# Moving one-operand work of an RWKV-7 / GLA encoder's recurrences from VectorE to ScalarE

## The chip, the cores and the metric

The kernel runs on one core of one Trainium2 chip. The metric is the device time of one execution in microseconds (us). TensorE (PE, with its weight loads PEld) multiplies, VectorE (DVE), ScalarE (ACT) and GpSimd (POOL) do elementwise work, and SyncE (SP) issues the transfers (DMA). Each engine takes its instructions in the order in which its list has them.

## The reference

One encoder layer is applied to two sequences, of 512 and 256 tokens, with 1024 channels in fp32. The mixer is the part that matters here: half of its channels go through an RWKV-7 recurrence (8 heads of 64, in both directions), half through gated linear attention (GLA, 4 heads, in both directions). A memory attention and a feed-forward layer follow.

```python
def rwkv7_scan(r, w, k, v, kk, a):               # per head, state S of 64 x 64
    def step(S, inp):
        r_t, w_t, k_t, v_t, kk_t, a_t = inp
        sa = jnp.einsum('bhij,bhj->bhi', S, -kk_t)
        S = (S * w_t[:, :, None, :] + sa[..., None] * (kk_t * a_t)[:, :, None, :]
             + v_t[..., None] * k_t[:, :, None, :])
        return S, jnp.einsum('bhij,bhj->bhi', S, r_t)
...
    kk = hd(k * p['k_k'])                        # scaled keys, then normalised per head
    kk = kk * lax.rsqrt(jnp.sum(kk * kk, axis=-1, keepdims=True) + 1e-12)
...
    a = jax.nn.sigmoid(a0 + ad @ a2)
    kd = hd(k * (1.0 + (a - 1.0) * k_a))         # decayed key, per direction
...
def encoder_trunk(x, mem, params):
        x = x + rms_norm(hybrid_mixer(rms_norm(x, p['g_mix_pre']), p), p['g_mix_post'])
        m = rms_norm(mem, p['g_mem'])
        x = x + rms_norm(cross_attention(rms_norm(x, p['g_x_pre']), m, p), p['g_x_post'])
        h = rms_norm(x, p['g_ffn_pre'])
        x = x + rms_norm(jnp.square(jax.nn.relu(h @ p['w_ff1'])) @ p['w_ff2'], p['g_ffn_post'])
```

## The kernel before

The 768 tokens stand side by side in tiles of 128 channels. A product in fp32 is made of three passes: each operand is split into a high part (ACT, L149) and a rest (DVE, L150), and `mm3` (L249) sums three products. A dense block is 128 columns of a weight: four transfers `wraw`, four splits `whi` and `wlo`, then 24 matmuls of 512 columns and 24 of 256, and an evacuation by ACT (L482 for GLA, L322 with two DVE passes L324 and L327 for the RWKV inputs). The tiles of the splits hold one block, so a block's splits follow the matmuls of the block before.

The recurrence is cut into chunks of 64 tokens and worked on by pairs of heads p = 0 to 3:

- `begin(p)`: `prep` makes the scaled and normalised key `kk` (L704, L705, head sums, L706 to L708). For each direction d `decays` makes the cumulated decays (L649 or L651 by a scan, L653, L655) and the decayed key (L659, L661, L662); `bk_of`, `ar_of` and `lower` make the chunk matrices (`low`, evacuated by L695) and send them through HBM.
- `invert(p)`: `inverses` loads 48 + 48 lower triangles of 32x32 (`sn`, `sx`), turns the second half end to end (L746), does 31 column steps on DVE (a product L752 and a sum L754 each), and stores the results: direct, transposed (L756, L760) and turned (L758).
- `joined(p)`: `join` loads these blocks (`tt`, `tdz`) and makes the 64x64 inverses by two products on PE (L796 with its copy L800, L808 with its copy L811).
- `stage(q)`: `step` runs the recurrence itself over chunks (L1046 to L1077), with `products` ahead of it.

Beside it run the four GLA heads (`gla_head(h)`, L848 to L947: decays, score products L872 `gs`, turn L885, states L900 and the DVE chain L911, outputs L923 and L925, store to `mixd`), the dense blocks and, after 1296 of their matmuls, the blocks of the memory (`memory_block`). `tokens_first` turns a 128-channel tile to tokens first, by PE, and copies the result to SBUF (L472).

The order is set by the framework: it gives every instruction a priority by its place in the program, raised in `tc.high_priority(offset=...)`, simulates all engines with a cost model, and writes down each engine's list in the order in which the simulation ran it. So an instruction that changes its engine can move others on all engines. Each list is then fixed, and a waiting instruction holds up what stands behind it. All transfers are issued by SP, from one list.

Of the kernel before, what the change touches and what calls it, by code (L numbers as in the profile page):

```python
# [10 lines left out]
AF = mybir.ActivationFunctionType  # L11
ALU = mybir.AluOpType
# [20 lines left out]
def kernel(ctx: ExitStack, tc: tile.TileContext, I, y_prompt, y_sample):  # L33
    nc = tc.nc
    act = nc.scalar
    dve = nc.vector
# [262 lines left out]
    ka1 = cp.tile([P, 4], F32, name="ka1")  # L299
# [15 lines left out]
    def cvc(name, i=0):  # L315
        return cv[:, col[name] + i:col[name] + i + 1]
# [73 lines left out]
    for v in ("w0_f", "w0_b", "a0_f", "a0_b", "k_k", "k_a", "lnx_w", "lnx_b"):  # L390
# [11 lines left out]
                      op0=ALU.mult, op1=ALU.add)  # L402
# [61 lines left out]
    def tokens_first(ot):  # L464

        vt = gd2("gd")
        for c, n in SEQS:
            pt = psd("gvt")
            for j in range(0, n, P):
                pe.transpose(out=pt[:, j:j + P], in_=ot[:, c + j:c + j + P], identity=ident)  # L470
            with tc.high_priority():
                dve.tensor_copy(out=vt[:, c:c + n], in_=pt[:, 0:n])  # L472
        return vt.rearrange("p (j e) -> p j e", e=P)

    def gla_dense(g, i):
# [12 lines left out]
    if True:  # L488
# [72 lines left out]
        with tc.high_priority(offset=3000):  # L561
            for p in range(4):
                cs = slice(p * P, (p + 1) * P)
                for kind in (0, 2):
                    ots = [lp.tile([P, T], F32, tag="lo", bufs=6, name="lo_t") for _ in range(2)]
                    wt, xt = (w2s, xw) if kind < 2 else (a2s, xa)
                    for c0, n in SEQS:
# [3 lines left out]
                        for d in range(2):  # L571
                            sigm = act.activation(out=ots[d][:, c0:c0 + n], in_=pts[d][:, 0:n], func=AF.Sigmoid,
                                                  bias=cvc(("w0_f", "w0_b", "a0_f", "a0_b")[kind + d], p))
# [4 lines left out]
                for c0, n in SEQS:  # L578
                    pt, pz = psy("lops"), psy("gzps")
# [16 lines left out]
        for i in range(4):  # L596
# [3 lines left out]
            for k0 in range(0, KD, 4):  # L600
                pt = psm("ptr")
# [23 lines left out]
    sn, sq, sx = snf[0:112], sqf[0:112], sxf[0:112]  # L625
# [16 lines left out]
    def decays(st, d):  # L642

        p = st["p"]
        wa = pt_("wa")
        dma(wa, lora[p, d])
        cum = pt_("wb")
        if d == 0:
            dve.tensor_tensor_scan(out=cum, data0=scan_mask, data1=wa, initial=0.0, op0=ALU.mult, op1=ALU.add)  # L649
        else:  # L650
            dve.tensor_tensor_scan(out=cum[:, ::-1], data0=scan_mask, data1=wa[:, ::-1], initial=0.0,  # L651
                                   op0=ALU.mult, op1=ALU.add)
        act.activation(out=px_at, in_=v3(cum), func=AF.Exp, scale=-E_HALF)  # L653
        pinv = pt_("wa")
        act.activation(out=pinv, in_=cum, func=AF.Exp, scale=E_HALF)  # L655
        wc = pt_("wc")
        dma(wc, lora[p, 2 + d])
        nka = pt_("wb")
        dve.scalar_tensor_tensor(out=nka, in0=wc, scalar=-1.0, in1=st["kk"], op0=ALU.mult, op1=ALU.mult)  # L659
        kd = st["kds"] if d == 0 else wc  # L660
        dve.tensor_scalar(out=wc, in0=wc, scalar1=cvc("k_a", p), scalar2=ka1[:, p:p + 1], op0=ALU.mult, op1=ALU.add)  # L661
        dve.tensor_tensor(out=kd, in0=wc, in1=st["k"], op=ALU.mult)  # L662
        return pinv, nka, kd

# [35 lines left out]
    def prep(st):  # L700

        p = st["p"]
        kk, wa = pt_("kk", 2), pt_("wa")
        act.activation(out=wa, in_=st["k"], func=AF.Square, scale=cvc("k_k", p))  # L704
        dve.tensor_scalar(out=kk, in0=st["k"], scalar1=cvc("k_k", p), scalar2=None, op0=ALU.mult)  # L705
        head_sums(wa, lambda c0, n, pt: act.activation(out=wa[:, c0:c0 + n], in_=pt[:, 0:n], func=AF.Ln, bias=eps_kk))  # L706
        act.activation(out=wa, in_=wa, func=AF.Exp, scale=-0.5)
        dve.tensor_tensor(out=kk, in0=kk, in1=wa, op=ALU.mult)  # L708
        st["kk"] = kk
        st["r"] = pt_("r")  # L710
        dma(st["r"], rkvd[p, 1])
        st["kds"] = pt_("kds")
        st["lts"] = []

        pcs = st["pcs"] = mp.tile([P, 6, 4], F32, tag="pcs", bufs=4, name="pcs")
        for d in range(2):
            pinv, nka, kd = decays(st, d)
            b_ = bk_of(pinv, nka, kd)
            to_places(bkd[p], b_, d)
            a_ = ar_of(st, d)  # L720
            to_places(ard[p], a_, d)
            lower(st, d, b_, a_)
            if d == 1:
                dve.tensor_tensor(out=st["kds"], in0=st["kds"], in1=kd, op=ALU.add)
            last = px[:, :, 1 if d else 64].rearrange("p (q c) -> p q c", c=2)
            for c, n in ((0, 6),) if d == 0 else ((0, 4), (4, 2)):
                o = pcs[:, c:c + n, 2 * d:2 * d + 2]
                pool.tensor_scalar(out=o[:, ::-1] if d else o, in0=last[:, c:c + n], scalar1=1.0, scalar2=None, op0=ALU.mult)
# [10 lines left out]
    def inverses(st):  # L739


        flat = fl
        ld, qd, td = (x[st["p"]] for x in (lds, qds, tds))
        dma(sn[0:48], ld[0].rearrange("s b c t -> (b c) s t"))
        dma(sx[64:112], ld[1].rearrange("s b c t -> (b c) s t"))
        dve.tensor_copy(out=flat(sn[64:112]), in_=flat(sx[64:112])[:, ::-1])  # L746
        dve.memset(sq, 0.0)
        dve.memset(flat(sq)[:, 0:1024:33], 1.0)
        for j in range(31):
            nr, ni = j + 1, 31 - j  # L750
            tm = stmp[:, 0:nr * ni].rearrange("p (a b) -> p a b", a=nr)
            dve.tensor_tensor(out=tm, in0=sq[:, 0:nr, j:j + 1].broadcast_to([112, nr, ni]),  # L752
                              in1=sn[:, j:j + 1, j + 1:32].broadcast_to([112, nr, ni]), op=ALU.mult)
            dve.tensor_tensor(out=sq[:, 0:nr, j + 1:32], in0=sq[:, 0:nr, j + 1:32], in1=tm, op=ALU.add)  # L754
        dma(qd[0].rearrange("s b c t -> (b c) s t"), sq[0:48])
        dve.tensor_copy(out=sn[0:48], in_=sq[0:48].rearrange("p a b -> p b a"))  # L756
        dma(td[0].rearrange("s b c t -> (b c) s t"), sn[0:48])
        dve.tensor_copy(out=flat(sx[64:112]), in_=flat(sq[64:112])[:, ::-1])  # L758
        dma(qd[1].rearrange("s b c t -> (b c) s t"), sx[64:112])
        dve.tensor_copy(out=sn[64:112], in_=sq[64:112, ::-1, ::-1].rearrange("p a b -> p b a"))  # L760
        dma(td[1].rearrange("s b c t -> (b c) s t"), sn[64:112])
    def begin(p, k_=None):
        if k_ is None:
# [16 lines left out]
    def join(st):  # L780
        qd, td = qds[st["p"]], tds[st["p"]]
        tt, lts = tts, st["lts"]
# [7 lines left out]
        for d in range(2):  # L790
            o0, o1 = 32 * d, 32 - 32 * d
# [10 lines left out]
        for d in range(2):  # L802
            o0, o1 = 32 * d, 32 - 32 * d
            pn = psn("merge2")[:, 0:NCH * 32].rearrange("p (c x) -> p c x", x=32)
            for c in range(NCH):
                for h in (0, 64):
                    ks_ = slice(h + o1, h + o1 + 32)
                    pe.matmul(out=pn[h + o0:h + o0 + 32, c, :], lhsT=fts[d][ks_, c, :], rhs=tt[d][ks_, c, o1:o1 + 32],  # L808
                              start=True, stop=True)
            for h in (0, 64):  # L810
                dve.tensor_copy(out=tt[d][h + o0:h + o0 + 32, :, o1:o1 + 32], in_=pn[h + o0:h + o0 + 32])  # L811
            to_places(ttd[st["p"]], tt[d], d)

    def blocks(bs):
# [518 lines left out]
    with tc.tile_pool(name="ao", bufs=1, reuse_waits="tile") as ao:  # L1333
# [18 lines left out]
        for h in range(4):  # L1352
# [16 lines left out]
            for s_, (c0, n) in enumerate(SEQS):  # L1369
# [19 lines left out]
                for m in range(2):  # L1389
                    pt = psm("xt")  # L1390
# [95 lines left out]
    with tc.tile_pool(name="f1", bufs=1, reuse_waits="tile") as f1, tc.tile_pool(name="fw", bufs=1, reuse_waits="tile") as fw:  # L1486
# [98 lines left out]
        h = {"11": blk[0][0], "21": blk[1][0], "22": blk[1][1], "t1": blk[0][1]}  # L1585
# [185 lines left out]
```

## Time and profile before

| | us |
|---|---|
| median of 3 runs | 1554.85 |
| lowest and highest of the runs | 1549.77 and 1558.52 |
| the profiled execution, its own time | 1548.75 |
| span of the profile, first to last instruction | 1546.6 |
| busy PE, weight load, DVE, ACT, POOL | 1408.3, 1183.6, 1076.7, 706.0, 220.9 |
| mean granted TensorE clock | 0.930 of full speed |

The times in the profile count from the span's start. "Busy" counts an engine's instructions and not its waits; a row's "idle before" names what ended a wait. The first preparation starts at some 118 us, the fourth inversion ends at some 650 us, and the mixer's output product starts at some 787 us.

### The profile page before, as it was taken

Reading aid. Unit: us, or ns where it says so; the run is one execution under the profiler, and the core shown is the slowest. Engines: PE = TensorE matmul, PEld = TensorE weight load, DVE = VectorE, ACT = ScalarE, POOL = GpSimd, SP = SyncE. Lnnn points to the kernel's source line nnn. Section 1 sums busy time; section 2 is a strip of 40 time slices with the busy share of each in tenths; the row PEclk is TensorE's granted clock in tenths of the full one; section 3 lists DMA queues with packets and bytes.
Section 4 is the critical chain, followed back from the end, with each engine's and each line's share of the span. In section 5 each row is a group of like instructions: output and inputs, shape, how many; then the busy total and the mean of one; then the engine's idle time right before and its main releaser. Section 6 shows DMA issues by size and latency. Waiting matters only on the chain.

```text
span 1546.6 us, 27578 instructions
## 1 busy us (share of the span) xinstructions
PE 1408.3 (91%) x10238; PEld 1183.6 (77%) x10238; DVE 1076.7 (70%) x1913; ACT 706.0 (46%) x1477; POOL 220.9 (14%) x304
## 2 busy tenths in 40 slices
PE   7998899897799987999699999978999999999996
PEld 6886778775676766777478887868999998787785
DVE  5555896698567994866665554279766667788886
ACT  5664345443423442344353454345554555454342
POOL 5301000000000000003211233320000002132132
PEclk9999899987779996799799999988999999999998
DMA  6687666584468667464452332244554547555334
GB/s 165 177 314 210 171 197 156 167 228 102 128 187 232 180 184 168 106 166 144 128 179 98 107 100 79 82 154 155 196 170 153 181 157 291 155 175 172 120 103 136
DMA packets 279562, 250.30 MB, mean 162 GB/s; under 512 B 89264, under 2 KB 227059, under 8 KB 279428
## 3 DMA queue, kind: packets, MB, share of 16 engines
q1 hardware_dynamic: 279428, 248.54, 53.8%
q8 instruction: 81, 1.33, 0.4%
q14 instruction: 53, 0.43, 0.1%
HBM read 164.11 MB, written 82.58 MB: 160 GB/s over the span
## 4 chain that ended last, share of the span: by engine, by line
PE 59%; DVE 13%; DMA 11%; issue 8%; SPq 3%; ACT 3%; POOL 2%; DVEq 0%; ACTq 0%; POOLq 0%
PE pd L249 19%; PE fx L1548 7%; PE gx L1548 6%; PE fz L1548 5%; PE gz L1548 5%; SPq L41 3%; PE po L249 3%; DMA wraw<-in_w_in_dram 1%; DVE ws L1488 1%; PE hsum L639 1%; DVE wl L1539 1%; DMA raw<-in_w_out_dram 1%; PE xo L249 1%; POOL rs L1264 1%; PE bktp L1028 1%
## 5 line engine op out<-in xcount | busy, mean ns | idle before, releaser
L249 PE MATMUL pd<-hT_hi,whi 128*128 128x256 f32 (+1 forms) x512 | 183.5, 358 | 9.1 <-DVE gd L327 4.1
L249 PE MATMUL pd<-hT_lo,whi 128*128 128x256 f32 (+1 forms) x512 | 180.2, 352 | 0.3 <-DVE hT_lo L208 0.3
L249 PE MATMUL pd<-hT_hi,wlo 128*128 128x256 f32 (+1 forms) x512 | 178.5, 350 | 0.0
L149 ACT ACTIVATE whi<-wraw 128x256 fp32r<-128x256 f32 x192 | 77.5, 415 | 97.2 <-PE pd L249 59.4
L249 PEld LDWEIGHTS pd<-hT_hi,whi 128*128 128x128 f32 x512 | 100.9, 197 | 24.0 <-DVE gd L327 4.0
L150 DVE TENSOR_TENSOR wlo<-wraw,whi 128x256 fp32r<-128x256 f32 x192 | 80.2, 437 | 48.2 <-ACT whi L149 46.6
L249 PEld LDWEIGHTS pd<-hT_lo,whi 128*128 128x128 f32 x512 | 101.0, 197 | 13.1 <-DVE hT_lo L208 0.5
L249 PEld LDWEIGHTS pd<-hT_hi,wlo 128*128 128x128 f32 x512 | 100.2, 196 | 13.2 <-issue 0.5
L150 DVE TENSOR_TENSOR ul<-ur,uh 128x768 fp32r<-128x768 f32 x56 | 75.3, 1351 | 30.2 <-ACT uh L149 17.7
L149 ACT ACTIVATE uh<-ur 128x768 fp32r<-128x768 f32 x56 | 47.2, 845 | 106.6 <-PE gz L1548 51.8
L1538 ACT ACTIVATE wh<-w 128x1024 fp32r<-128x1024 f32 x64 | 67.1, 1053 | 36.7 <-PE fz L1548 24.2
L1539 DVE TENSOR_TENSOR wl<-w,wh 128x1024 fp32r<-128x1024 f32 x56 | 68.2, 1217 | 15.3 <-ACT wh L1538 14.7
L1548 PE MATMUL gx<-wh,uh 128*128 128x512 f32 x192 | 74.9, 397 | 4.2 <-DVE acc L1741 4.2
L1548 PE MATMUL gx<-wl,uh 128*128 128x512 f32 x192 | 75.9, 395 | 0.0
L1548 PE MATMUL gx<-wh,ul 128*128 128x512 f32 x192 | 75.4, 395 | 0.0
L1539 POOL TENSOR_TENSOR wl<-w,wh 128x1024 fp32r<-128x1024 f32 x8 | 20.9, 2610 | 329.3 <-ACT wh L1538 329.3
L1548 PE MATMUL fz<-hh,wh 128*128 128x384 f32 x192 | 66.1, 344 | 1.7 <-ACT wh L1538 1.7
L1548 PE MATMUL fz<-hl,wh 128*128 128x384 f32 x192 | 65.9, 343 | 0.0
L1548 PE MATMUL fz<-hh,wl 128*128 128x384 f32 x192 | 65.2, 344 | 0.6 <-DVE wl L1539 0.6
L1538 ACT ACTIVATE wh<-ws 128x1024 fp32r<-128x1024 f32 x48 | 50.5, 1052 | 27.2 <-PE fx L1548 22.5
L1548 PE MATMUL gz<-wl,uh 128*128 128x512 f32 x144 | 56.9, 395 | 0.0
L249 PE MATMUL pd<-mem_hi,wlo 128*128 128x512 f32 x128 | 56.0, 439 | 0.9 <-DVE wlo L150 0.9
(537 smaller groups left out, 3980.4 us busy)
## 6 DMA issues: line engine op xcount, KB each, us to landing
w<-in_w_ff_dram SPq DMA_DIRECT2D x64, 512.0 KB
ur<-ud SPq DMA_DIRECT2D x56, 384.0 KB
wraw<-in_w_in_dram SPq DMA_DIRECT2D x108, 128.0 KB
ud<-u SPq DMA_DIRECT2D x32, 384.0 KB
ud<-us SPq DMA_DIRECT2D x24, 384.0 KB
wraw<-in_wkv_x_dram SPq DMA_DIRECT2D x64, 128.0 KB
lora<-lo_t SPq DMA_DIRECT2D x20, 384.0 KB
bkg<-bkd SPq DMA_DIRECT2D x24, 256.0 KB
```

Source lines behind the costliest of these rows:

```text
L41: return nc.sync.dma_start(out=out, in_=in_)
L149: act.activation(out=hi, in_=src, func=AF.Copy)
L150: (lo_eng or pool).tensor_tensor(out=lo, in0=src, in1=hi, op=ALU.subtract)
L249: pe.matmul(out=out, lhsT=a, rhs=b, start=(i == 0), stop=(i == n - 1))
L639: pe.matmul(out=pt[:, 0:n], lhsT=ones_bd, rhs=src[:, c0:c0 + n], start=True, stop=True)
L1028: pe.transpose(out=pt[:, u, :], in_=fl(b_[HS[h], u]), identity=ident[HS[h], HS[h]])
L1264: pool.tensor_tensor(out=rs, in0=ms, in1=neg_half, op=ALU.pow)
L1488: dve.tensor_tensor(out=out, in0=a, in1=b, op=ALU.subtract)
L1538: act.activation(out=hi, in_=t[name], func=AF.Copy)
L1539: lo_eng.tensor_tensor(out=lo, in0=t[name], in1=hi, op=ALU.subtract)
L1548: pe.matmul(out=out, lhsT=a, rhs=b, start=first and i == 0, stop=last and i == n - 1, skip_group_check=True)
```

## The change

Eight lines of five functions are written for ACT instead of DVE. Seven copies, of which four read or write turned or transposed, are ACT's Copy; the scaled key is Copy with a column as scale; the decayed key's factor is Identity with a column as scale and one as bias. Shapes, tiles, transfers and results are the same; no table is loaded more often.

```diff
 tokens_first:
-                dve.tensor_copy(out=vt[:, c:c + n], in_=pt[:, 0:n])
+                act.activation(out=vt[:, c:c + n], in_=pt[:, 0:n], func=AF.Copy)
 decays:
-        dve.tensor_scalar(out=wc, in0=wc, scalar1=cvc("k_a", p), scalar2=ka1[:, p:p + 1], op0=ALU.mult, op1=ALU.add)
+        act.activation(out=wc, in_=wc, func=AF.Identity, scale=cvc("k_a", p), bias=ka1[:, p:p + 1])
 prep:
-        dve.tensor_scalar(out=kk, in0=st["k"], scalar1=cvc("k_k", p), scalar2=None, op0=ALU.mult)
+        act.activation(out=kk, in_=st["k"], func=AF.Copy, scale=cvc("k_k", p))
 inverses:
-        dve.tensor_copy(out=flat(sn[64:112]), in_=flat(sx[64:112])[:, ::-1])
+        act.activation(out=flat(sn[64:112]), in_=flat(sx[64:112])[:, ::-1], func=AF.Copy)
...
-        dve.tensor_copy(out=sn[0:48], in_=sq[0:48].rearrange("p a b -> p b a"))
+        act.activation(out=sn[0:48], in_=sq[0:48].rearrange("p a b -> p b a"), func=AF.Copy)
...
-        dve.tensor_copy(out=flat(sx[64:112]), in_=flat(sq[64:112])[:, ::-1])
+        act.activation(out=flat(sx[64:112]), in_=flat(sq[64:112])[:, ::-1], func=AF.Copy)
...
-        dve.tensor_copy(out=sn[64:112], in_=sq[64:112, ::-1, ::-1].rearrange("p a b -> p b a"))
+        act.activation(out=sn[64:112], in_=sq[64:112, ::-1, ::-1].rearrange("p a b -> p b a"), func=AF.Copy)
 join:
-                dve.tensor_copy(out=tt[d][h + o0:h + o0 + 32, :, o1:o1 + 32], in_=pn[h + o0:h + o0 + 32])
+                act.activation(out=tt[d][h + o0:h + o0 + 32, :, o1:o1 + 32], in_=pn[h + o0:h + o0 + 32], func=AF.Copy)
```

The lines keep their numbers. What the scheduler makes of it is seen at three places. The first is ACT at the first GLA head's start, while the last of the first dense blocks are split and evacuated (`arena` are the head's tiles, L848 takes its first transfer, L857 its scans; `gd` <- `pd` is a block's evacuation, `gd` <- `gvt` the copy of `tokens_first`). Before:

```order
L848 ACTIVATE arena<-arena 128x768
L849 ACTIVATE arena<-arena 128x768
L706 ACTIVATE wa<-hsum,eps_kk 128x256
L850 ACTIVATE arena<-arena,ones_f 128x768
L707 ACTIVATE wa<-wa 128x768
L482 ACTIVATE gd<-pd 128x512
L149 ACTIVATE whi<-wraw 128x256 x2
L857 ACTIVATE arena<-arena 128x768
L858 ACTIVATE arena<-arena 128x768
L149 ACTIVATE whi<-wraw 128x256 x2
L482 ACTIVATE gd<-pd 128x256
```

and now, at the same place:

```order
L848 ACTIVATE arena<-arena 128x768
L707 ACTIVATE wa<-wa 128x768
L482 ACTIVATE gd<-pd 128x512
L149 ACTIVATE whi<-wraw 128x256
L849 ACTIVATE arena<-arena 128x768
L149 ACTIVATE whi<-wraw 128x256 x3
L482 ACTIVATE gd<-pd 128x256
L472 ACTIVATE gd<-gvt 128x512
L850 ACTIVATE arena<-arena,ones_f 128x768
L472 ACTIVATE gd<-gvt 128x256
L653 ACTIVATE px<-wb 128x12x64
L655 ACTIVATE wa<-wb 128x768
```

The second evacuation and all four splits have moved ahead of L857 (which now comes next), and the two copies L472 stand there too.

The second place is ACT after the first preparation's last chunk matrix (`lsb` <- `low`). Before:

```order
L695 ACTIVATE lsb<-low 128x512
L695 ACTIVATE lsb<-low 128x256
L149 ACTIVATE whi<-wraw 128x256 x3
L929 ACTIVATE arena,ss<-go 128x128 x4
L932 ACTIVATE ss<-ss,eps_gla 128x4
```

and now:

```order
L695 ACTIVATE lsb<-low 128x512
L695 ACTIVATE lsb<-low 128x256
L746 ACTIVATE snf<-sxf 48x1024
L322 ACTIVATE gd<-pd,mu_111 128x512
L149 ACTIVATE whi<-wraw 128x256 x4
```

L746, which takes what has gone out from `lsb` and come back, stands between L695 and the next evacuation and splits.

The third place is DVE at the end of the fourth GLA head (L911 its state chain, L942 and L947 its output) and of the second inversion (L752, L754). Before, the last L911 stands 15 rows ahead of this piece:

```order
L752 TENSOR_TENSOR stmp<-sqf,snf 112x87
L754 TENSOR_TENSOR sqf<-sqf,stmp 112x29x3
L752 TENSOR_TENSOR stmp<-sqf,snf 112x60
L754 TENSOR_TENSOR sqf<-sqf,stmp 112x30x2
L752 TENSOR_TENSOR stmp<-sqf,snf 112x31
L754 TENSOR_TENSOR sqf<-sqf,stmp 112x31
L756 COPY snf<-sqf 48x1024
L758 COPY sxf<-sqf 48x1024
L760 COPY snf<-sqf 48x1024
L942 TENSOR_TENSOR arena<-arena 128x768
L947 SCALAR_TENSOR_TENSOR arena<-got,cv,arena 128x512
```

and now:

```order
L754 TENSOR_TENSOR sqf<-sqf,stmp 112x29x3
L911 SCALAR_TENSOR_TENSOR arena<-arena,dec 64x128 x3
L752 TENSOR_TENSOR stmp<-sqf,snf 112x60
L911 SCALAR_TENSOR_TENSOR arena<-arena,dec 64x128 x2
L754 TENSOR_TENSOR sqf<-sqf,stmp 112x30x2
L911 SCALAR_TENSOR_TENSOR arena<-arena,dec 64x128
L752 TENSOR_TENSOR stmp<-sqf,snf 112x31
L754 TENSOR_TENSOR sqf<-sqf,stmp 112x31
L942 TENSOR_TENSOR arena<-arena 128x768
L947 SCALAR_TENSOR_TENSOR arena<-got,cv,arena 128x512
```

The inversion's last steps and the head's last L911 now end side by side, and the three copies are gone from this list. On SP the store of this head's output (`mixd`) stands, before and now, behind that inversion's stores and the loads of the join. On PE the last two dense blocks of the first 1296 matmuls stood one on each side of this head's score products; now both stand ahead of them. Of the 192 products L1046 of the recurrence 64 stood behind or within the last ten dense matmuls; now 100 do.

## The prediction

> **What bounds the kernel now.** I read the page first for the engines' shares, then the table of busy time by stretch, then the chain that ended last and the list in order of time at the places where TensorE stands still. The page's first line says that TensorE (PE) carries most of the span:
>
> ```profile
> PE 1408.3 (91%) x10238; PEld 1183.6 (77%) x10238; DVE 1076.7 (70%) x1913; ACT 706.0 (46%) x1477; POOL 220.9 (14%) x304
> ```
>
> All edited lines run between 100 and 790 us, so only that part counts. In the table by stretch a row has the stretch, its length, then busy us (instructions) of PE, weight load, DVE, ACT and POOL, then the granted clock, the DMA share and GB/s:
>
> ```profile
> 100.00:139.00 39.00, 38.34 (x237) 33.39 (x236) 16.79 (x32) 21.82 (x43) 3.02 (x4) 1.00 0.95 280
> 139.00:147.00 8.00, 0.89 (x5) 0.32 (x3) 7.66 (x9) 3.10 (x7) 3.01 (x3) 0.77 0.69 181
> 147.00:360.00 213.00, 195.82 (x1542) 158.20 (x1543) 176.75 (x343) 94.02 (x232) 11.98 (x35) 0.92 0.64 178
> 360.00:402.00 42.00, 20.60 (x231) 15.05 (x229) 28.00 (x74) 17.43 (x56) 0.00 (x0) 0.60 0.45 109
> 402.00:500.00 98.00, 90.78 (x836) 70.95 (x833) 64.46 (x130) 33.15 (x82) 0.69 (x3) 0.87 0.71 194
> 500.00:580.00 80.00, 74.31 (x693) 56.98 (x691) 74.35 (x180) 34.15 (x84) 0.98 (x3) 0.95 0.62 178
> ...
> 610.00:650.00 40.00, 36.78 (x431) 27.98 (x431) 37.91 (x121) 12.80 (x41) 0.00 (x0) 0.69 0.46 131
> 650.00:790.00 140.00, 124.48 (x1704) 93.96 (x1705) 91.37 (x248) 61.28 (x172) 24.12 (x42) 0.90 0.54 153
> 790.00:1547.00 757.00, 715.86 (x3628) 630.00 (x3626) 516.83 (x666) 360.15 (x630) 141.44 (x156) 0.98 0.45 147
> ```
>
> The reader should see three things. VectorE (DVE) is as full as PE at 500 to 580 (74.35 of 80) and at 610 to 650 (37.91 of 40): there a shorter DVE list can help. ScalarE (ACT) is never over 60% busy, so its capacity is no limit; its order can be. And PE has two real holes, 139 to 147 (0.89 busy of 8) and 360 to 402 (20.60 of 42). Nothing in the last row is edited: 757 us stay as they are.
>
> **The change, part by part.** What leaves DVE (shortest, median and longest ns of one instruction):
>
> ```profile
> L472 DVE COPY gd<-gvt x16: 406/542/692, 106.9 to 448.3; 128x512 f32<-128x512 f32 x8, 128x256 f32<-128x256 f32 x8
> L661 DVE TENSOR_SCALAR wc<-wc,cv,ka x8: 666/676/680, 150.6 to 550.5; 128x768 f32<-128x768 f32 x8
> L705 DVE TENSOR_SCALAR kk<-k,cv x4: 614/616/620, 120.9 to 498.7; 128x768 f32<-128x768 f32 x4
> L746 DVE COPY snf<-sxf x4: 691/691/691, 194.4 to 607.9; 48x1024 f32<-48x1024 f32 x4
> L756 DVE COPY snf<-sqf x4: 1032/1072/1101, 242.1 to 647.2; 48x1024 f32<-48x1024 f32 x4
> L758 DVE COPY sxf<-sqf x4: 691/692/693, 243.2 to 648.3; 48x1024 f32<-48x1024 f32 x4
> L760 DVE COPY snf<-sqf x4: 1045/1082/1123, 243.8 to 648.9; 48x1024 f32<-48x1024 f32 x4
> L811 DVE COPY tt<-merge x16: 539/553/565, 264.0 to 674.3; 32x384 f32<-32x384 f32 x16
> ```
>
> That is 8x0.69+8x0.41 for L472, 8x0.676 for L661, 4x0.616 for L705, 4x(0.691+1.072+0.692+1.082) for the inversions and 16x0.553 for L811: 8.8+5.4+2.5+14.1+8.8 = 39.6 us off DVE. What they cost on ACT is priced by ACT's own groups of like size (busy us, mean ns, then idle before):
>
> ```profile
> L482 ACT ACTIVATE gd<-pd 128x512 f32<-128x512 f32 x12 | 7.1, 595 | 34.1 <-PE pd L249 29.1 <-issue 5.0
> L482 ACT ACTIVATE gd<-pd 128x256 f32<-128x256 f32 x12 | 4.4, 368 | 2.3 <-PE pd L249 2.2
> L322 ACT ACTIVATE gd<-pd,mu 128x512 f32<-128x512 f32 x10 | 6.9, 688 | 26.0 <-PE pd L249 18.0 <-issue 8.0
> L655 ACT ACTIVATE wa<-wb 128x768 f32<-128x768 f32 x8 | 6.6, 827 | 0.0
> L800 ACT ACTIVATE sqf<-merge 32x384 f32<-32x384 f32 x16 | 7.7, 482 | 16.2 <-PE merge L796 16.0
> L1538 ACT ACTIVATE wh<-w 128x1024 fp32r<-128x1024 f32 x64 | 67.1, 1053 | 36.7 <-PE fz L1548 24.2 <-PE fx L1548 9.9 <-PE gz L1548 1.8
> ```
>
> L322 is L482 with a column as its scale, so a column costs 688-595 = 93 ns. Then L472 is 8x0.595+8x0.368 = 7.7, L661 with two columns 8x(0.827+0.186) = 8.1, L705 4x0.92 = 3.7, the sixteen inversion copies 16x1.053 = 16.8, L811 16x0.482 = 7.7: 44.0 us. No row shows ACT reading with a stride or backwards as the inversion copies do; the contiguous 1.053 is one end, and twice that the other (DVE's own worst ratio here is 1.082 to 0.691, 1.6). I take 1.053, the row of the same length. Busy time itself moves nothing off the path; the terms are places.
>
> The Trainium skill, "ScalarE: Activation LUTs", Rules for kernel authors, says to give additions and multiplications to VectorE and not to ScalarE; "Perfetto Trace Analysis", Optimizing Scalar/DVE Operations, allows the move where DVE is saturated. The trace bears both: the same work is 44.0 against 39.6, and DVE is saturated only in two of nine stretches. By the first rule alone the sum would be +4.4 us; it is a rival below.
>
> *Term 1, the hole at 139 to 147.* In order of time:
>
> ```profile
> 134.34 0.86 ACT arena L848
> ...
> 140.02 0.54 SPq L41 DMA_DIRECT2D wa<-lora  x1
> ...
> 142.57 0.84 ACT L857 ACTIVATE arena<-arena 128x768 f32<-128x768 f32 x1 [3.49 <-DVE arena L854]
> 145.08 0.69 PE L470 MATMUL gvt<-ident,gd 128*128 128x128 f32 x2 [5.90 <-ACT gd L482]
> 146.98 0.80 PE L249 MATMUL pd<-hT_hi,whi 128*128 128x512 f32 x1 [1.21 <-DVE gd L472]
> ```
>
> PE waits for the evacuation L482, which stands on ACT behind L857, which waits for two scans on DVE; then for L472, which stands on DVE behind a third. In the new order L482 and both halves of L472 stand ahead of L857, on the same engine, so neither waits for a scan. They stand behind L848 instead, whose input is now issued some five transfers later (I put 3 us on that, from the 0.54 that SP takes for one). From 137.3: L848, L707, L482, a split, L849, three splits, L482, L472 come to 0.86+0.83+0.6+0.42+0.83+1.25+0.37+0.6 = 5.8, so PE resumes near 143 and not 147: **-4.0**, between 0 and the whole 7.1 us.
>
> *Term 2, L746 in front of the first inversion.*
>
> ```profile
> 185.74 0.38 ACT L695 ACTIVATE lsb<-low 128x256 f32<-128x256 f32 x1 [0.78 <-PE low L693]
> 194.36 0.70 DVE snf L746
> 213.12 10.85 PE pd L249 x48
> ```
>
> L746 waits for a trip through HBM that starts when L695 has ended: 194.36-186.12 = 8.2 us. In the new order it stands on ACT right behind that L695, and behind it are the evacuation L322 and the four weight splits of the next block. They come at 8.2+1.05+0.69+0.42, plus 0.44 for DVE's half of a split: 10.8 us after L695. PE has meanwhile the larger part of one block, 24 steps of 512 and 24 of 256, some 8.3 us of the 10.85 that a whole block with its evacuation stalls takes: **+2.5**, between 0 (a full block ahead of it) and +8.2 (none). At the other three inversions a dozen or more instructions stand between L695 and L746; I cost those at nothing, covered by these, and 8.2 each if that cover is gone.
>
> *Term 3, the hole at 360 to 402.*
>
> ```profile
> 372.86 0.36 DVE arena L911
> ...
> 379.75 0.21 DVE L754 TENSOR_TENSOR sqf<-sqf,stmp 112x31 f32<-112x31 f32 x1
> 386.99 1.14 DVE L947 SCALAR_TENSOR_TENSOR arena<-got,cv,arena 128x512 f32<-128x512 f32 x2
> 392.92 2.75 DMA mixd<-arena
> ```
>
> The result of the fourth GLA head is ready at 388.13, but its store goes out at 392.9: on SP it stands behind the stores and loads of the second inversion, which ends 6.7 us after the last L911. In the new order the inversion ends right behind the last L911, so SP is through before L947 is: **-4.7**, or 0 if something else holds SP. Against it, all dense blocks now stand ahead of that head's score products, which before ran beside one:
>
> ```profile
> 351.79 0.62 PE gs L872 x32
> 353.17 0.81 PE gkt L885 x6
> ```
>
> Exposed are the 48 products (the 32 take 0.62, so about 1.3 with their gaps), the turn L885 and its two evacuations on ACT (0.97): **+3.0**, or 0 if DVE was late anyway. The three inversion copies cost 0.3 more on ACT than on DVE, and L800, which waits for the join, now stands ahead of L940: **+0.8**, at most 3.
>
> *Term 4, DVE where it is full.* At 500 to 580 two L661 and one inversion's end leave it (1.35+2.85), at 610 to 650 one inversion's end and two L811 (2.8+0.9): 7.9 us. PE idles 5.7+3.2 = 8.9 there. Half is my estimate, since the waits there alternate between DVE, DMA and PE: **-4.0**, between 0 and -7.9.
>
> *Term 5, the tail.* In the new order 100 of the 192 products of L1046 stand behind nearly all dense work, in the old one 64. Three rounds more run without filler:
>
> ```profile
> 722.56 0.23 PE rec L1046 x8
> ...
> 725.04 0.38 PE rec L1046 x8
> ```
>
> A round takes some 2.5 to 3 us and fills PE there, so most of it only moves; a quarter of 8.6 is my estimate: **+2.0**, between 0 and +8.6.
>
> L705 lies beside the head sum (L639) that its user waits for anyway; L661 beside the six products that DVE does from other tiles (its cost if uncovered: 8x0.34 = 2.7). Both cost nothing.
>
> The sum is -4.0+2.5-4.7+3.0+0.8-4.0+2.0 = **-4.4 us**. The profiled execution took 1548.75 us, 6.1 below the median of the runs, 1554.85; the same step from the median gives **1550 us**.
>
> **The rivals.** *DVE's relief goes through in full.* For it: nearly half of the 39.6 us leave DVE before 360, where PE has further holes. Against: PE is busy 195.8 of 213 there. Term 1 at 7.1, term 4 at 7.9, term 3 without its price and some 5 us of the 17 idle at 147 to 360: 7.1+7.9+4.7+5 less 2.5+2.0 is about -20: 1535 us.
>
> *ScalarE's order becomes the wait* (the other side). ACT feeds PE with weight splits, and now also waits in line for PE, DVE and HBM at L472, L746 and L756. If the three later L746 stall ACT too, or L756 waits for an inversion that is late, each costs up to 8.2 less a few us of cover, say 5: term 2 at 8.2 and three times 5 is +23, less the -8 or so that the gains then still bring: 1555+15 = 1570. It decides from about 4 us per inversion on. For it: the first one is certain. Against: the other three have rows in between.
>
> *The move only costs.* By the skill's first rule the total grows; by the rows above by 4.4 us, if DVE's relief is hidden and ACT's time is not: 1559 us.
>
> *It changes nothing* because another engine's wait takes over in each place: 1555 us.
>
> **How the numbers follow.** 0.5% of the median is 7.8 us, about what a measurement of this kernel can tell from no change: 1547.1 to 1562.6 is the same. My forecast has a chance of 0.45, with a range of its own of 1541 to 1559, so 0.16 of it faster and 0.29 the same. Full relief 0.25, all faster. ACT's order 0.18, nearly all slower. Move only costs 0.05, half slower; nothing changes 0.07, the same with a little over on both sides. Together faster 0.42, same 0.36, slower 0.22. The range from the first rival to the third, 1534 to 1568, leaves about 2 in 10 out.
>
> **What would show it.** Term 1: no PE hole of over 4 us before the first head's scores. Term 2: an ACT wait of 8 us at L746, once, and PE short of weights right after. Term 3: the fourth store of mixd goes out under 1 us after L947. Term 4: DVE under 90% where the third and fourth inversions run. Term 5: more us between the last memory block and the first output product. Wrong it would be if ACT waits at L746 or L756 three or four times, or if a new order puts PE behind a late transfer at a place that I did not look at: PE's rows are largely reordered, and each such place is worth 3 to 5 us here.

## The result and the profile after

The kernel after takes 1563.36 us (median of 20 runs, 1560.04 to 1574.44) against 1554.93 us (20 runs, 1548.71 to 1567.42): a ratio of 1.0051, 95% interval 1.0031 to 1.0071. It is slower by half a per cent, 8.4 us. The time lies inside the predicted range, just past the 1562.6 us at which the prediction lets "the same" end; the direction is the one that I held unlikeliest. Below, ratios are always to the kernel before run on the same chip and go by undisturbed runs, while medians take in disturbed ones too. 0.1% is 1.55 us.

The profiled execution of after has a span of 1559.8 us. The page's line of engines:

```profile
PE 1407.0 (90%) x10238; PEld 1186.0 (76%) x10238; DVE 1036.8 (66%) x1853; ACT 749.4 (48%) x1537; POOL 221.1 (14%) x304
```

DVE has lost 39.9 us and ACT has gained 43.4; I had worked out 39.6 and 44.0. The second agreement is luck: the eight lines by themselves are busy for 51.8 us on ACT, since half of the inversion copies take twice what I took (below), and ACT's busy time grows by less because neighbours in its list overlap: in after one L655 starts at 176.31, while the L653 before it, from 175.56 for 0.84 us, ends at 176.40. PE has the same work, so what was added is time in which it stands still. The table by stretch of after, in the cuts of the prediction:

```profile
139.00:147.00 8.00, 5.19 (x18) 3.85 (x18) 4.25 (x7) 5.05 (x13) 0.00 (x0) 0.79 1.00 281
147.00:360.00 213.00, 186.95 (x1424) 151.32 (x1423) 157.69 (x307) 105.92 (x244) 11.21 (x30) 0.89 0.61 167
360.00:402.00 42.00, 29.02 (x242) 22.24 (x240) 26.22 (x65) 23.84 (x55) 3.99 (x8) 0.72 0.47 117
402.00:500.00 98.00, 78.30 (x731) 63.29 (x733) 60.83 (x126) 36.41 (x87) 0.69 (x3) 0.79 0.65 174
500.00:580.00 80.00, 71.43 (x737) 53.12 (x731) 66.22 (x156) 39.15 (x90) 0.87 (x3) 0.98 0.71 205
610.00:650.00 40.00, 40.00 (x523) 30.84 (x522) 36.56 (x122) 17.59 (x49) 0.00 (x0) 0.99 0.46 130
650.00:790.00 140.00, 116.92 (x1725) 90.25 (x1722) 80.72 (x228) 59.01 (x164) 24.62 (x42) 0.83 0.49 140
```

PE is busier in the two holes that I looked at (5.19 against 0.89, 29.02 against 20.60) and idler in the stretches between them: 8.9 us less at 147 to 360, 12.5 less at 402 to 500 (a part of this is the same work coming later).

The two spans differ by 13.2 us, the medians by 8.4. The last output product tells where the rest is; first before, then after, in the answer on the tile `po`:

```profile
L249 PE MATMUL po<-w_pl,mix_lsb x36: 391/397/478, 792.4 to 844.8; 128*128 128x512 f32 x36
```

```profile
L249 PE MATMUL po<-w_pl,mix_lsb x36: 391/398/496, 804.7 to 853.1; 128*128 128x512 f32 x36
```

Up to there after is 8.3 us late. Behind it, where nothing edited runs, the two executions take 1546.6-844.8 = 701.8 and 1559.8-853.1 = 706.7 us; I take the difference for scatter between two executions, since the medians differ by 8.4.

Who waits for whom shows where much of the 8 us arises. The chain of a preparation is: the load `wa`<-`lora`, the scan L649 or L651 on DVE, the exponentials L653 and L655 on ACT. In the list of waits (engine, line, who ended the wait: us, times, longest) of before, 100 to 850 us:

```profile
ACT px L653 <- DVE wb L649: 5.4, 3, 2.4
DVE wb L651 <- DMA wa<-lora: 3.6, 3, 1.6
ACT px L653 <- DVE wb L651: 3.5, 3, 1.7
PE gds L900 <- ACT arena L903: 1.6, 3, 0.7
```

and of after:

```profile
ACT px L653 <- DVE wb L649: 16.7, 4, 6.8
ACT snf L746 <- DMA sxf<-ld: 15.7, 4, 8.3
ACT px L653 <- DVE wb L651: 14.4, 4, 9.1
DVE wb L651 <- DMA wa<-lora: 13.9, 4, 6.8
ACT snf L756 <- DVE sqf L754: 10.6, 4, 4.9
PE gds L900 <- ACT arena L903: 10.1, 5, 6.6
```

ScalarE waits 31.1 us at L653 where it waited 8.9, and TensorE waits 10.1 us for L903 where it waited 1.6. L653 is not an edited line, and no term of my sum is about it. ScalarE also waits at every one of the four moved L746 and the four moved L756; what those are worth, the experiments tell. The longest of the waits at L653, in order of time in after:

```profile
157.97 0.94 DVE L864 SCALAR_TENSOR_TENSOR arena<-arena 128x768 f32<-128x768 f32 x1
161.91 0.94 DVE L866 TENSOR_TENSOR arena<-arena,dec 128x768 f32<-128x768 f32 x1
163.74 0.95 DVE L674 TENSOR_TENSOR bk<-kds,wa 64x768 f32<-64x768 f32 x1
166.97 0.65 SPq L41 DMA_DIRECT2D wa<-lora  x1
173.70 1.76 DVE L651 TENSOR_TENSOR_SCAN wb<-scan_mask,wa 128x768 f32<-128x768 bf16 x1 [6.80 <-DMA wa<-lora]
175.56 0.84 ACT L653 ACTIVATE px<-wb 128x768 f32<-128x768 f32 x1 [9.09 <-DVE wb L651]
178.22 0.58 ACT L902 ACTIVATE arena<-gds 64x512 f32<-64x512 f32 x1
179.36 1.22 PE L900 MATMUL gds<-arena 64*128 64x128 f32 x4 [6.59 <-ACT arena L903]
```

and in before:

```profile
159.96 0.95 DVE L674 TENSOR_TENSOR bk<-kds,wa 64x768 f32<-64x768 f32 x1
163.88 0.64 SPq L41 DMA_DIRECT2D wa<-lora  x1
165.84 0.59 ACT L902 ACTIVATE arena<-gds 64x512 f32<-64x512 f32 x1 [2.35 <-PE gds L900]
169.50 1.76 DVE L651 TENSOR_TENSOR_SCAN wb<-scan_mask,wa 128x768 f32<-128x768 bf16 x1 [0.53 <-DMA wa<-lora]
171.35 0.85 ACT L653 ACTIVATE px<-wb 128x768 f32<-128x768 f32 x1 [1.73 <-DVE wb L651]
```

`wa` has one buffer. The load for the second direction has to wait until L674 has read the first direction's values out of it. In after, L674 ends 3.8 us later, because the GLA head's products that L857 and L858 feed (L863, L864, L866) now stand among the products of the preparation on DVE; in before they were done by 149.7 us. The load goes out 3.1 us later. And on ACT two pairs of evacuations L902 and L903 (of the GLA head's state products L900) stood ahead of L653 before, while now they stand behind it (with the evacuation L322 and two weight splits). So ACT waits 9.09 us for the scan, and PE 6.59 us for ACT. That hole gives back what the hole at 139 had gained. Behind two further waits of ScalarE at L653, 6.84 us until 297 and 5.52 until 433, TensorE is idle for 3.7 us until 299, waiting for L149, and for 4.0 until 439, waiting for a product of L653's result.

### The profile page after: what moved, and what is told of

The parts are those of the page before. It is cut to its first block, busy times and chain, and to the rows that moved or that the text cites. A ratio compares the mean times of both kernels' runs of the same rounds, so it can differ in the third digit from the quotient of the medians.

```text
span 1559.8 us, 27582 instructions
## 1 busy us (share of the span) xinstructions
PE 1407.0 (90%) x10238; PEld 1186.0 (76%) x10238; DVE 1036.8 (66%) x1853; ACT 749.4 (48%) x1537; POOL 221.1 (14%) x304
## 4 chain that ended last, share of the span: by engine, by line
PE 54%; DVE 16%; DMA 11%; issue 9%; ACT 4%; SPq 3%; POOL 2%; DVEq 0%; ACTq 0%; POOLq 0%
PE pd L249 15%; PE fx L1548 7%; PE gx L1548 6%; PE fz L1548 5%; PE gz L1548 5%; SPq L41 3%; PE po L249 3%; DMA wa<-lora 2%; PE xo L249 1%; PE hsum L639 1%; DVE wlo L150 1%; DMA wraw<-in_w_in_dram 1%; PE xs L249 1%; DVE ws L1488 1%; DMA raw<-in_w_out_dram 1%
## 5 line engine op out<-in xcount | busy, mean ns | idle before, releaser
L249 PEld LDWEIGHTS pd<-hT_hi,wlo 128*128 128x128 f32 x512 | 100.1, 196 | 13.2 <-issue 0.5
L149 ACT ACTIVATE whi<-wraw 128x256 fp32r<-128x256 f32 x192 | 75.4, 412 | 72.2 <-PE pd L249 39.5
L149 ACT ACTIVATE uh<-ur 128x768 fp32r<-128x768 f32 x56 | 47.3, 846 | 107.6 <-PE gz L1548 51.9
L1538 ACT ACTIVATE wh<-w 128x1024 fp32r<-128x1024 f32 x64 | 67.1, 1052 | 37.9 <-PE fz L1548 24.2
L1538 ACT ACTIVATE wh<-ws 128x1024 fp32r<-128x1024 f32 x48 | 50.5, 1052 | 27.3 <-PE fx L1548 22.3
L1548 PE MATMUL gz<-wh,uh 128*128 128x512 f32 x144 | 56.1, 396 | 1.1 <-ACT uh L149 1.1
```

The lines of the kernel that those rows point to most:

```text
L149: act.activation(out=hi, in_=src, func=AF.Copy)
L249: pe.matmul(out=out, lhsT=a, rhs=b, start=(i == 0), stop=(i == n - 1))
L1538: act.activation(out=hi, in_=t[name], func=AF.Copy)
L1548: pe.matmul(out=out, lhsT=a, rhs=b, start=first and i == 0, stop=last and i == n - 1, skip_group_check=True)
```

## The experiments

The change does two things at once: it moves work to another engine, and it makes the scheduler write every engine's list anew. To part them I fixed the lists. A kernel is traced once with one set of lines on ScalarE, to get its order, and once more with another set, where every instruction gets an edge to its predecessor on its engine that orders the issue and waits for nothing:

```diff
+names = build(inputs, lines_of_the_order)[2]      # the other kernel's order
+nc = build(inputs, lines_on_scalare, order=names)
 ...
+for n in order:
+    i = byname[n]
+    if i.engine in last:
+        tc.add_manual_dep(i, last[i.engine], DependencyInfo(NoSync, DATA), reason="order")
+    last[i.engine] = n
```

A moved instruction stands in its new engine's list at the place where the other kernel's common order has it. In the traces of these runs every unmoved instruction of VectorE and ScalarE stands in the fixed order. No run fixes a kernel's own order with its own lines, so what the fixing costs by itself is not measured.

**Order against engine.** All eight lines on ScalarE in the order of before, none in the order of after, and the sixteen inversion copies (L746, L756, L758, L760) alone in both.

```diff
-order of after, L472 L661 L705 L746 L756 L758 L760 L811 on ScalarE
+order of before, L472 L661 L705 L746 L756 L758 L760 L811 on ScalarE
```

> All eight edited lines run on ScalarE as after the change, but every engine's list keeps the order of the kernel before (the moved instructions stand in ScalarE's list where the old list of all engines had them). Theory 'order' (the 8 us come from the new order that the scheduler made of all the lists): the loss is gone, 1549 to 1557 us, since only the moved work's price (about +4) and VectorE's relief (about -4) are left. Rival 'engine' (the 8 us are the work on ScalarE itself: longer copies and waits in line at L746 and L756): the loss stays, 1561 us or more, whatever the order.

Measured: 1.0003 (0.9971 to 1.0036), 1554.2 us.

```diff
-order of after, all eight lines on ScalarE
+order of after, none of the eight lines on ScalarE
```

> The counterpart: all eight lines run on VectorE as before, but every engine's list keeps the order of the kernel after. Theory 'order': still slower, 1561 to 1568 us. Rival 'engine': back at 1555 us.

Measured: 1.0124 (1.0085 to 1.0162), 1574.1 us. The order loses 1.24% by itself, 19 us, more than the whole change; the work on ScalarE then wins a part of it back. "Engine" alone is refuted.

```diff
-order of after, all eight lines on ScalarE
+order of after, L472 L661 L705 L811 on ScalarE
```

> Order of the kernel after; only the sixteen copies of the four inversions (L746, L756, L758, L760) go back to VectorE, the other edits stay on ScalarE. 'Engine' through the inversions (8 us of waiting at the first L746, 2.0 instead of 1.07 us for each of the eight turned copies): 1555 to 1558 us. 'Order': 1561 to 1566 us, no change from the kernel after.

Measured: 1.0029 (1.0000 to 1.0059), between the two expectations: 0.2% under the kernel after, which is no more than these intervals can tell.

```diff
-order of before, none of the eight lines on ScalarE
+order of before, L746 L756 L758 L760 on ScalarE
```

> Order of the kernel before; only the sixteen inversion copies run on ScalarE. 'Engine' through the inversions: 1559 to 1564 us. 'Order': 1553 to 1557 us, within half a per cent of the kernel before.

Measured: 1.0072 (1.0037 to 1.0108), 1562.2 us. Here "engine" was right: the inversion copies alone lose 11 us on ScalarE. So both theories hold a part, and the other four lines must gain.

**The parts of the work, in the order of before.**

```diff
-order of before, none of the eight lines on ScalarE
+order of before, L472 L661 L705 L811 on ScalarE
```

> Order of the kernel before; L472, L661, L705 and L811 on ScalarE, the sixteen inversion copies on VectorE. In that order all eight lines cost nothing together (1554.2) and the inversion copies alone cost 8.0 (1562.2). Theory 'two parts': the inversion copies lose 8 us and the four others gain 8: 1546 us (1542 to 1550). Rival 'saturated': the copies cost something only where VectorE still carries the rest, and the rest gains nothing alone: 1553 to 1556 us.

Measured: 0.9921 (0.9890 to 0.9953). The four lines gain 12 us; "saturated" is refuted.

```diff
-order of before, all eight lines on ScalarE
+order of before, L472 L661 L705 L811 L746 L758 on ScalarE
```

> Order of the kernel before; everything on ScalarE except the two turned copies of each inversion (L756, L760), which stand at the end of the inversion, took 1.07 us each on VectorE and 2.0 us on ScalarE, and have the stores and the join behind them. Theory 'strided reads': 4 x 2 x 0.93 = 7.4 us come off the path of the four joins: 1547 us (1544 to 1550). Rival 'waiting in line at L746': that stays on ScalarE here, so 1552 to 1556 us.

Measured: 0.9971 (0.9942 to 1.0000). It lies between all eight (1.0003) and the four (0.9921), and between the two expectations. Taken at their middles, L756 and L760 (the transposed copies, which the expectation calls turned) are about 0.3% of the inversions' 0.8%, L746 and L758 the other 0.5%; each half is hardly more than the intervals, so this run does not decide between long reads and waiting in line.

The durations are plain. By line, in after:

```profile
L746 ACT ACTIVATE snf<-sxf x4: 1053/1058/1059, 195.5 to 594.6; 48x1024 f32<-48x1024 f32 x4
L756 ACT ACTIVATE snf<-sqf x4: 1957/2006/2047, 244.6 to 649.2; 48x1024 f32<-48x1024 f32 x4
L758 ACT ACTIVATE sxf<-sqf x4: 1053/1057/1057, 246.6 to 651.2; 48x1024 f32<-48x1024 f32 x4
L760 ACT ACTIVATE snf<-sqf x4: 1940/2031/2065, 247.6 to 652.2; 48x1024 f32<-48x1024 f32 x4
```

and one place where they cost is plain too: the end of the second inversion, in order of time, with the inversion copies alone on ScalarE:

```profile
384.73 0.21 DVE L754 TENSOR_TENSOR sqf<-sqf,stmp 112x31 f32<-112x31 f32 x1
388.08 0.93 ACT L940 ACTIVATE arena<-arena,ones_f 128x768 f32<-128x768 f32 x1
389.16 1.93 ACT L756 ACTIVATE snf<-sqf 48x1024 f32<-48x1024 f32 x1
393.09 1.94 ACT L760 ACTIVATE snf<-sqf 48x1024 f32<-48x1024 f32 x1
395.05 0.30 SPq L41 DMA_DIRECT2D td<-snf  x1
```

against before, where the last L754 ends at 379.96 (quoted in the prediction) and the last store goes out at

```profile
383.47 1.85 SPq L41 DMA_DIRECT2D td<-snf  x1
```

From the last step of the inversion to its last store it is 10.1 us and was 3.5: L756 stands 4.2 us in line behind the fourth GLA head's work on ACT, and the three copies themselves take 2.2 us longer.

```diff
-order of before, none of the eight lines on ScalarE
+order of before, L472 L811 on ScalarE
```

> Order of the kernel before; only the evacuations L472 and L811 on ScalarE (17.6 of the 25.5 us that the four lines take off VectorE; L661 and L705 stay there). Theory 'evacuations': they carry most of the 8 us that the four lines gain together: 1547 to 1550 us. Rival 'the keys' (L661 and L705 are what VectorE is rid of in the preparations): 1553 to 1556 us.

Measured: 0.9998 (0.9962 to 1.0034). The evacuations alone bring nothing that can be seen, against the expectation that they carry most of the gain.

```diff
-order of before, none of the eight lines on ScalarE
+order of before, L661 L705 on ScalarE
```

> Order of the kernel before; only L661 and L705 on ScalarE. Theory 'the keys': since L472 and L811 alone bring nothing (1553.3), these bring the gain of the four lines, 1546 to 1549 us, though they are only 7.9 us of VectorE's time. Rival 'together only': the gain needs all four, 1552 to 1556 us.

Measured: 0.9978 (0.9940 to 1.0016). Neither pair alone shows the gain of the four; whether it needs all four, or is the two small ones added up, these intervals leave open.

**The wait at L653.** The same lists as the kernel after, with the load's wait taken away: a buffer of its own for the rates, and their eight loads eleven places sooner on SP.

```diff
-        wa = pt_("wa")
-        dma(wa, lora[p, d])
+        wa = pt_("wl")
+        dma(wa, lora[p, d])              # 11 places sooner in SP's list
...
-        kk, wa = pt_("kk", 2), pt_("wa")
+        kk, wa = pt_("kk"), pt_("wa")
```

> Assignment and order of the kernel after, with one wait removed: the rates that the scans L649 and L651 read are loaded into a buffer of their own (kk has one buffer instead of two for it), and their eight loads are issued 11 places sooner on SP; nothing else moves. Theory 'ScalarE in line at L653': in the kernel after, the scans wait 21 us in all for these loads, ScalarE waits 31 us at L653 for the scans, and the evacuations and weight splits behind L653 leave TensorE idle at 179 (6.6), 299 (3.7), 439 (4.9) and 457 (2.5): most of these 17.7 us go, 1548 to 1556 us. Rival 'the order costs in many other places': 1560 to 1565 us.

Measured: 0.9941 (0.9916 to 0.9967), 1547.1 us: 1.1% under the kernel after, about 17 us, and faster than before. In its list of waits

```profile
ACT px L653 <- DVE wb L649: 9.3, 4, 4.2
ACT px L653 <- DVE wb L651: 5.8, 3, 3.6
PE gds L900 <- ACT arena L903: 4.4, 5, 1.5
```

ScalarE waits 15.1 us at L653 instead of 31.1, and in order of time

```profile
157.33 0.64 SPq L41 DMA_DIRECT2D wl<-lora  x1
165.56 1.76 DVE L651 TENSOR_TENSOR_SCAN wb<-scan_mask,wl 128x768 f32<-128x768 bf16 x1
167.41 0.85 ACT L653 ACTIVATE px<-wb 128x768 f32<-128x768 f32 x1 [3.58 <-DVE wb L651]
173.41 0.71 PE L900 MATMUL gds<-arena 64*128 64x128 f32 x4 [1.48 <-ACT arena L903]
```

the scan no longer waits, and the hole of 6.59 us is one of 1.48. That the late loads carry the loss is shown by this run. That they do so through ScalarE in line at L653 is read from the rows and not shown apart: the edit also takes away VectorE's own waits for these loads, and it changes the buffers and the place on SP together. With the same early loads:

```diff
-order of after, early loads, all eight lines on ScalarE
+order of after, early loads, none of the eight lines on ScalarE
```

> All eight lines on VectorE, order of the kernel after, and the scans' loads in their own buffer and 11 places sooner. Without the early loads this order took 1574.1 us. Theory 'the order loses through the late loads alone': back to 1554 to 1559 us. Rival 'it loses in many places, and the early loads are worth some 16 us less here since VectorE is fuller': 1564 to 1570 us.

Measured: 1.0023 (0.9993 to 1.0053). Of the order's 1.24%, 1.0% goes with the early loads: nearer to "the late loads alone" than to the rival, and ScalarE's wait at L653 falls here too, from 31.3 us to 16.4.

```diff
-order of after, early loads, all eight lines on ScalarE
+order of after, early loads, L472 L661 L705 L811 on ScalarE
```

> The order of the kernel after with the early loads (1547.1), and the sixteen inversion copies back on VectorE. Theory 'the inversion copies cost wherever they stand' (5 to 12 us in the order of before, some 3 in the order of after): 1540 to 1545 us. Rival 'with ScalarE no longer in line they are covered': 1546 to 1549 us.

Measured: 0.9904 (0.9872 to 0.9937), 1541.4 us. It is the lowest ratio of the study, though its interval overlaps that of the four lines in the order of before (0.9921). Against 0.9941 the inversion copies cost 0.4% here, hardly more than the intervals.

```diff
-order of before, L472 L661 L705 L811 on ScalarE
+order of before, L472 L661 L705 L811 on ScalarE, early loads
```

> The first kernel of these four (order of before, L472, L661, L705, L811 on ScalarE), with the eight loads into a buffer of their own and 10 places sooner. The scans of the kernel before wait 10.8 us in all for them, mostly beside other work: 0 to 6 us under the first of these four, 1540 to 1547 us if that comes to 1546. If the waits are all covered, the same as the first.

Measured: 0.9922 (0.9889 to 0.9955), the same as without (the loads are ten places sooner here). ScalarE's wait at L653 falls from 10.0 us to 5.0 and the time stays: in the old order these waits are covered.

**What the scheduler makes by itself.** Without fixed lists:

```diff
-all eight lines on ScalarE
+L472 L661 L705 L811 on ScalarE
```

> L472, L661, L705 and L811 on ScalarE, the inversion copies on VectorE, and the scheduler makes its own order. In that order L653 stands ahead of the same instructions as in the kernel after at its first two and its last four places (ahead of L322, L149 and L902 at the second). Theory 'order' (ScalarE in line at L653): much of the loss stays, 1553 to 1561 us. Rival 'the four lines gain in any order': 1545 to 1550 us, as in the order of before.

Measured: 1.0023 (0.9980 to 1.0065); its runs scatter widely (1548 to 1580 us). The gain of the four lines (0.9921) is gone in that order, as "order" said, and ScalarE waits 28.6 us at L653 there.

```diff
 all eight lines on ScalarE
-        wa = pt_("wa")
+        wa = pt_("wl")                   # own buffer; kk has one
```

> All eight lines on ScalarE, the rates of the scans in a buffer of their own (kk with one), and the scheduler makes its own order; it issues those loads sooner by itself. Theory 'late loads with ScalarE in line behind them': faster than the kernel after by most of what the early loads gave in its order (16 us), 1546 to 1556 us. Rival 'any new order costs': 1560 us or more.

Measured: 0.9938 (0.9910 to 0.9966), 1546.6 us. With nothing changed beside the two buffers (one more for the rates, one less for `kk`) the scheduler's own order is 1.1% under the kernel after.

```diff
 none of the eight lines on ScalarE
-        wa = pt_("wa")
+        wa = pt_("wl")                   # own buffer; kk has one
```

> The kernel before with the scans' rates in a buffer of their own (kk with one), and the scheduler's own order; none of the eight lines is moved. Theory 'the change made this wait': the kernel before has evacuations ahead of L653, so little to gain, 1550 to 1557 us, slower than the same kernel with the eight lines on ScalarE (1546.6). Rival 'the early loads are the whole gain': 1545 to 1549 us.

Measured: 0.9984 (0.9949 to 1.0019). The buffer gives the kernel before little or nothing; it is the changed kernel that needs it. ScalarE waits 20.4 us at L653 in this run, more than the 8.9 of before, and loses nothing: TensorE's wait for L903 is 1.1 us. A sum of waits is no price; what counts is what stands behind the wait.

```diff
 L472 L661 L705 L811 on ScalarE
-        wa = pt_("wa")
+        wa = pt_("wl")                   # own buffer; kk has one
```

> L472, L661, L705 and L811 on ScalarE, the inversion copies on VectorE, the scans' rates in a buffer of their own, and the scheduler's own order. Theory: as in the order of after with early loads (1541.4), 1539 to 1546 us. Rival 'the inversion copies are covered in the scheduler's own order': the same as with all eight lines, 1546 to 1549 us; or its order makes a new wait: 1550 us or more.

Measured: 0.9945 (0.9914 to 0.9976), the same as with all eight. The 1539 to 1546 us that I expected did not come. Whether the inversion copies are covered in the scheduler's own order, or its new order makes another wait that eats their gain, this run leaves open.

## Why the prediction was wrong

Along one path of runs the change divides into the order, +1.24%, the four lines in it, -0.95% (1.0124 to 1.0029), and the inversion copies, +0.22% (1.0029 to 1.0051, within the intervals); together +0.51%, as the steps of any path must. Along the other path the four lines come first, -0.79% (0.9921), then the inversion copies, +0.82% (to 1.0003), then the order, +0.48% (to 1.0051): what the order costs depends on where the work stands. That the result lies inside the range is luck as far as the sum goes, since it is the difference of a loss and a gain that were both larger than the terms.

**The step that failed** is the one that made the sum out of places: "Busy time itself moves nothing off the path; the terms are places", and then five places. The new order's dearest place, ScalarE in line at L653 behind a late load, was not among them. The loads that it waits for are worth 1.0 to 1.25% in three assignments of the work (1.0124 to 1.0023, 1.0029 to 0.9904, 1.0051 to 0.9941), 16 to 19 us, where the sum had nothing. The third rival had the mechanism, ScalarE's order becoming the wait, and 1570 us, but named L746 and L756, which the change moves, and not L653, which it only displaces. Both signs that the prediction named for being wrong came: ScalarE waits at L746 and at L756 four times each (15.7 and 10.6 us), and PE stands behind a late transfer at a place that I did not look at. The second carries the loss; the first is cheap in this order, since moving all sixteen inversion copies back is worth 0.2 to 0.4%. *The move only costs* came nearest by its number, 1559, but not by its mechanism: the work alone, in the order of before, costs nothing that can be seen (1.0003).

Point by point:

- **Term 1** was right by itself. The answer on PE in order of time in after:

```profile
140.28 0.66 PE L470 MATMUL gvt<-ident,gd 128*128 128x128 f32 x4 [1.19 <-ACT gd L482]
142.51 0.44 PE L470 MATMUL gvt<-ident,gd 128*128 128x128 f32 x2 [1.57 <-ACT gd L482]
```

  The hole is 2.76 us and was 7.11: -4.35, predicted -4.0. Its price, missing in the term, is what moved behind: the products on DVE that L857 feeds come later, and with them L674, the load, the scan and L653.
- **Term 2** was right for the first inversion: ScalarE waits 8.34 us at L746 and PE then 2.36 us. The other three waits at L746, which I put at nothing, come to 7.4 us together.

```profile
195.51 1.06 ACT L746 ACTIVATE snf<-sxf 48x1024 f32<-48x1024 f32 x1 [8.34 <-DMA sxf<-ld]
200.40 0.47 PE L249 MATMUL pd<-hT_hi,whi 128*128 128x512 f32 x1 [2.36 <-DVE gd L327]
```

  What was mis-sized is the rest of the inversion copies. I took 1.053 us for each of the sixteen and had 2.1 as the upper end; the eight of L746 and L758 take 1.06, the eight of L756 and L760 take 2.0. With that and the waiting in line the sixteen copies cost 0.7 to 0.8% in the order of before (1.0003 against 0.9921, 1.0072 against 1), 11 to 13 us, and 0.2 to 0.4% in the order of after, where I had +3.3 in terms 2 and 3.
- **Term 3**: the store of the fourth head's output does go out right behind its last L947:

```profile
402.79 1.14 DVE L947 SCALAR_TENSOR_TENSOR arena<-got,cv,arena 128x512 f32<-128x512 f32 x2
403.95 0.34 SPq L41 DMA_DIRECT2D mixd<-arena  x1
```

  0.02 us after it, where it was 4.8. But the head itself ends at 403.93 and not 388.13, and its score products L872 start at 373.25 and not 351.79, with one dense block more ahead of them and the delays from before. Whether the sooner store saves any time is not shown. The term's +3.0 for the exposed products fits: from 373.25 to 376.73 PE runs only the 48 products and the turn, and then waits. Its +0.8 (at most 3) for the copies was too small: from the last step of the inversion to its last store it is 10.3 us in after and was 3.5.
- **Term 4** was right in sign and too small. DVE is at 83% at 500 to 580 (66.22 of 80, under the 90% that I named) and at 91% at 610 to 650; PE gains there only in the second (40.00 against 36.78). But the four lines are worth 0.8 to 1.2% at equal order, 12 to 18 us, where I had -4.0 and at most -7.9, of which 5.6 were inversion copies (in the order of before that is without the gain of term 1, which comes from the order). So they gain outside the two full stretches too; where, these runs do not show. (The prediction's own table has a third full stretch, 139 to 147 with DVE busy for 7.66 of 8 us, which its "two of nine" left out.) The first rival (full relief, 1535) had this; with the early loads, and the inversion copies back on VectorE, the kernel comes to 1541.
- **Term 5**: the first output product (at 769 us in before, and not at the 787 given among the times before) starts at

```profile
L249 PE MATMUL po<-w_out,mix_bk x72: 387/392/1037, 769.1 to 839.7; 128*128 128x512 f32 x72
```

  in before and in after at

```profile
L249 PE MATMUL po<-w_out,mix_bk x72: 387/395/793, 775.5 to 848.0; 128*128 128x512 f32 x72
```

  6.4 us later; the last step of the last inversion comes 2.2 us later (646.7 and 648.9). By these two executions the tail costs 4.2 us, predicted +2.0 with 8.6 as its end.
- **L661 and L705 at nothing**: not contradicted (0.9978 with them alone).
- **The rival by the rule**: the Trainium skill, "ScalarE: Activation LUTs", Rules for kernel authors, gives additions and multiplications to VectorE. Only L661 and L705 are such work; the other six lines are copies. For these two the trace agrees on the duration, 1.02 and 0.93 us on ScalarE against 0.68 and 0.62 on VectorE, and yet moving them costs no time that can be seen (0.9978). The rival's price did not come out of the work: the four lines together gain on ScalarE at equal order, though L661 and L705 take longer there.

## What to carry to other kernels

Moving instructions between engines makes a scheduler rewrite every list, and an unedited instruction that waits for a load can come to stand ahead of the work that feeds the busiest engine; after such a change the list of waits is to be read for every line of the engine that got the work, not for the moved lines only, and together with what stands behind each wait. Fixing the lists of the other kernel parts order from work in two runs, and here they pulled against each other: +1.2% and -0.7%. Where an in-order engine stands behind a late load, give the load a buffer of its own with the move: in this kernel the buffer alone brought little or nothing (0.9984), the move alone lost (1.0051), and both together gained (0.9938 in the scheduler's own order, 0.9904 in the best fixed one).

## What the runs showed of the hardware

ScalarE read 1024 float32 elements per partition backwards as fast as forwards (1.057 us at L746 and L758, 1.053 in the contiguous group L1538 of before), but 1.94 to 2.07 us when neighbours in its reading order lie 32 elements apart (L756, L760): 0.93 ns more for each. VectorE lost less by the same pattern, 1.03 to 1.12 against 0.69 us. The Trainium skill, "SBUF — State Buffer", in the section on the DMA port swizzle, says that the memory has lines of 16 bytes and that each access to a new line pays a penalty, without a figure for either engine; the two durations agree with that.
